# The recurrence's states by single VectorE instructions, smaller quad steps in another order, and new step estimates

## The chip, the cores and the metric

The kernel runs on one core of a Trainium2 chip. The metric is the device time of one execution, in microseconds (us); lower is better. TensorE is called PE here, VectorE DVE, ScalarE ACT, GpSimd POOL, and SyncE, which issues most of the transfers, SP. Each engine takes its instructions strictly in its own order.

## The reference, cut to what matters

One decoder layer on 2048 tokens of width 1024. Eight heads do dilated sliding-window attention in three branches (dilations 1, 4 and 16); eight heads do a gated linear recurrence (HGRN2); both are projected out, and a mixture of 32 experts follows. The change is in the recurrence:

```python
def hgrn2(q, f_raw, i_in, lb):
    """f = lb + (1-lb)*sigmoid(f_raw); S_t = diag(f_t) S_{t-1} + (1-f_t) outer i_t; o_t = S_t^T q_t."""
    ...
    A = jnp.where(causal, jnp.einsum('bnthk,bnshk->bnhts', q_in, k_in), 0.0)
    o_intra = jnp.einsum('bnhts,bnshv->bnthv', A, vc)
    dS = jnp.einsum('bnshk,bnshv->bnhkv', k_end, vc)
    decay = jnp.exp(b_last[:, :, 0])
    def step(S_prev, inp):
        dec, ds = inp
        return dec[..., None] * S_prev + ds, S_prev
    _, S_prevs = lax.scan(step, S0, ...)
    o_inter = jnp.einsum('bnthk,bnhkv->bnthv', q_in, S_prevs)
    return (o_intra + o_inter).reshape(B, S, H, Dv)
```

## The kernel before

The first part (phase A) goes over four **pairs** of heads, each an attention pair with a recurrence pair. On PE a pair consists of: 16 `v` steps (`v_tile`), 32 q/k projection steps (`qk_chunk`), 64 `h` steps (`h_tile`, four to each of 16 token tiles), 48 score steps S (`scores`), 48 value steps P (`values`), and four **quads** of recurrence (`quad_steps`, four tiles each). A quad has the PE steps `decays` (d), `states` (s), `turns` (t), `within` (a) and `outputs` (o), after `gates`, which has no PE work. The second part (phase B, from about 1133 us) projects out and routes; the third (from about 1410 us) runs the experts.

PE's order is the order in which the program is written, and a greedy planner writes it: `Step(fn, cost, after, at)` has an estimated cost and a list of (earlier step, latency) in ns; `Runner.run` keeps a planned time and takes, from lists in a fixed rank (quad steps H first, then weights G, attention A, ..., projections F last), the first step whose predecessors have ended long enough ago. The estimates decide the order alone; at run time semaphores decide. The other engines' orders are made by the framework's scheduler from priorities. `h` steps of quad q wait in the planner for `outputs` of quad q-2 (`hgrn_steps`; `hq` has two buffers).

All quad steps and the weight norms (`w_scale`, PE step w) draw their PSUM tiles from one ring of two banks, `hg`. So a step can start only when the tile before the last one has been read out: by ACT for `states` (dS), `turns` (kT, kept in `key`, and qT) and the two exponentials of `decays`, by DVE for `within` (`copy_predicated` into `Am`).

In `states` each of the two chunks' dS is read out of PSUM by two ACT instructions. Then the recurrence goes eight steps: POOL scales the whole 128x128 state into `sw` (L658), DVE adds dS times the decay in two 64x64 halves (L661), and the next step's POOL instruction needs both. The states lie as 128x128 blocks in `Sp`, whose off-diagonal halves are zero; `outputs` reads `Sp` and `Am`.

`combine` (16 token blocks of branch 2 in pairs, eight calls to a pair of heads) loads the other two branches' rows into `R` by two SP transfers (L506), works on them with DVE (first L511, last L532) and POOL (L529, L531), and stores to `mix` by SP (L534). `R` has two buffers.

## Time and profile before

| what | value |
|---|---|
| median of 3 runs (lowest, highest) | 2217.72 us (2206.78, 2219.48) |
| the profiled execution's own time | 2217.23 us |
| its span, first to last instruction | 2215.3 us |
| mean granted PE clock | 0.943 |

The span lies 1.9 us below the time of the same execution, and that time within 0.5 us of the median. The rows that the prediction uses stand further down. In the strip of slices, each digit is the tenth of a slice (55 us); PEclk is the granted PE clock in tenths of 2.4 GHz, so that 5 is 1.2 GHz.

### The profile page before, as it was taken

Reading aid. Unit: us, or ns where it says so; the run is one execution under the profiler, and the core shown is the slowest. Engines: PE = TensorE matmul, PEld = TensorE weight load, DVE = VectorE, ACT = ScalarE, POOL = GpSimd, SP = SyncE. Lnnn points to the kernel's source line nnn. Section 1 sums busy time; section 2 is a strip of 40 time slices with the busy share of each in tenths; the row PEclk is TensorE's granted clock in tenths of the full one; section 3 lists DMA queues with packets and bytes.
Section 4 is the critical chain, followed back from the end, with each engine's and each line's share of the span. In section 5 each row is a group of like instructions: output and inputs, shape, how many; then the busy total and the mean of one; then the engine's idle time right before and its main releaser. Section 6 shows DMA issues by size and latency. Waiting matters only on the chain. (4 is left out here: it accounts for less than half of the span.)

```text
span 2215.3 us, 39749 instructions
## 1 busy us (share of the span) xinstructions
PE 1967.0 (89%) x13753; PEld 1345.8 (61%) x13777; DVE 1493.8 (67%) x4121; ACT 1201.4 (54%) x2646; POOL 567.3 (26%) x620
## 2 busy tenths in 40 slices
PE   4998978999899998899888998699999999999981
PEld 4645565555655556455444445569999977766750
DVE  6657787767857777567887677756656656556525
ACT  6455653765547655566554343456556655555524
POOL 2303244123431335411431112212233222111110
PEclk9998988998999998999899998799999999999995
DMA  7333254532535324553578995799999999999857
GB/s 229 85 94 96 66 128 112 114 90 70 118 101 123 83 75 113 174 119 71 128 168 226 290 253 164 253 353 315 312 311 314 329 315 313 325 325 321 302 149 299
DMA packets 438896, 433.37 MB, mean 196 GB/s; under 512 B 242644, under 2 KB 325716, under 8 KB 438176
## 3 DMA queue, kind: packets, MB, share of 16 engines
q1 hardware_dynamic: 420464, 382.74, 56.7%
q0 software_dynamic: 14064, 46.46, 8.5%
q8 instruction: 109, 1.79, 0.3%
q10 hardware_dynamic: 4160, 1.58, 0.3%
q14 instruction: 99, 0.81, 0.1%
HBM read 305.30 MB, written 66.29 MB: 168 GB/s over the span
## 5 line engine op out<-in xcount | busy, mean ns | idle before, releaser
L1660 DVE TENSOR_TENSOR eL<-eraw,eH 128x1024 bf16<-128x1024 f32 x248 | 298.0, 1218 | 107.9 <-ACT eH L1654 97.0
L1654 ACT ACTIVATE eH<-eraw 128x1024 fp32r<-128x1024 f32 x252 | 258.4, 1053 | 123.8 <-PE acc L1745 48.8
L453 ACT ACTIVATE P<-S,orow,fqk 128x256 f32<-128x256 f32 (+1 forms) x384 | 195.0, 512 | 172.3 <-DVE orow L447 94.1
L567 PE MATMUL proj<-whh,x 128*128 128x512 f16 x512 | 202.4, 395 | 0.1
L568 PE MATMUL proj<-whl,x 128*128 128x512 f16 x512 | 200.1, 391 | 0.0
L569 PE MATMUL proj<-whh,x 128*128 128x512 f16 x512 | 199.5, 390 | 0.0
L1726 PE MATMUL acc<-xs,eH 128*128 128x352 f32 (+15 forms) x1216 | 195.2, 313 | 1.8 <-DVE xs L1704 1.8
L436 PE MATMUL S<-k,qs 128*128 128x256 f16 (+1 forms) x768 | 172.4, 355 | 13.9 <-ACT P L453 10.9
L1726 PEld LDWEIGHTS acc<-xs,eH 128*128 128x128 f32 x1216 | 176.2, 190 | 4.7 <-issue 2.2
L440 DVE CUSTOM_DVE_ANT_0 S<-S,bias 128x256 f32<-128x256 f32 (+1 forms) x384 | 141.4, 369 | 54.8 <-PE S L436 51.6
L456 DVE TENSOR_TENSOR Ps<-P,Ps 128x256 f16<-128x256 f32 (+1 forms) x192 | 129.7, 675 | 68.8 <-ACT Ps L455 67.2
L1828 POOL DMA_INDIRECT x2d<-yo,sidx x49 | 105.2, 2146 | 255.7 <-DVE yo L1803 95.8
L1776 PE MATMUL acc<-hs,eD 128*128 128x176 f32 (+15 forms) x1216 | 165.1, 295 | 4.9 <-DVE ts L1751 3.0
L1776 PEld LDWEIGHTS acc<-hs,eD 128*128 128x128 f32 x1216 | 161.1, 190 | 6.0 <-DVE ts L1751 3.9
L1687 POOL DMA_INDIRECT xg<-h2d,gidx x49 | 56.1, 1146 | 334.0 <-PE tr L1701 159.6
L436 PEld LDWEIGHTS <-qs 128*128 128x128 f16 x768 | 89.5, 123 | 69.3 <-issue 20.3
L260 POOL TENSOR_TENSOR wraw<-wraw,g 128x1024 f32<-128x1024 f32 x44 | 84.7, 1928 | 167.8 <-DMA wraw<-in_w_in_dram 134.5
L1744 PE MATMUL acc<-eH,xs 128*128 128x512 f32 x208 | 118.4, 569 | 0.0
L1788 PE MATMUL acc<-eD,hs 128*128 128x512 f32 x208 | 98.0, 609 | 21.2 <-ACT yo L1801 11.5
L386 PE MATMUL proj<-wh,x 128*128 128x128 f16 x512 | 96.5, 231 | 18.9 <-DVE V L394 18.9
L455 ACT ACTIVATE Ps<-P 128x256 f16<-128x256 f32 (+1 forms) x192 | 102.8, 536 | 7.6 <-DMA PT<-Ps 5.0
L658 POOL TENSOR_SCALAR sw<-Sp,hw 128x128 f32<-128x128 f32 x112 | 53.3, 476 | 196.5 <-DVE Sp L661 106.5
(396 smaller groups left out, 4891.6 us busy)
## 6 DMA issues: line engine op xcount, KB each, us to landing
eraw<-in_w_gate_dram SPq DMA_DIRECT2D x128, 512.0 KB, 7.1
eD<-in_w_down_dram SPq DMA_DIRECT2D x128, 512.0 KB, 6.4
eraw<-in_w_up_dram SPq DMA_DIRECT2D x124, 512.0 KB, 6.3
wraw<-in_w_in_dram SPq DMA_DIRECT2D x41, 512.0 KB, 4.1
od<-orow SPq DMA_DIRECT2D x64, 132.0 KB, 2.0
R<-od SPq DMA_DIRECT2D x64, 132.0 KB, 2.4
xt<-in_x_dram SPq DMA_DIRECT2D x16, 512.0 KB, 4.8
wraw<-in_w_out_dram SPq DMA_DIRECT2D x16, 512.0 KB, 4.1
```

Source lines behind the costliest of these rows:

```text
L436: nc.tensor.matmul(ps[:, h, :W], q, self.block_cols(D['k'][h][:, x], br, blk, True), start=(x == 0), stop=(x == 1))
L440: nc.vector.tensor_tensor_reduce(ps[:, h, :W], ps[:, h, :W], bias[:, 256 - W:256], 1.0, -3.0e38, OP.add, OP.max, mx[:, h:h + 1])
L453: nc.scalar.activation(P[:, h], ps[:, h, :W], AF.Exp, bias=nm[:, h:h + 1], scale=f[:, h:h + 1], accum_out=orow[:, 130 + h:131 + h])
L456: nc.vector.tensor_tensor(hv[:, 1], P, hv[:, 0], op=OP.subtract)
L567: nc.tensor.matmul(ps, self.XH[n // 4][:, k, ns], W['whh'][:, k, :], start=(k == 0), stop=False)
L568: nc.tensor.matmul(ps, self.XH[n // 4][:, k, ns], W['whl'][:, k, :], start=False, stop=False)
L569: nc.tensor.matmul(ps, self.XL[n // 4][:, k, ns], W['whh'][:, k, :], start=False, stop=(k == KT - 1))
L1654: nc.scalar.activation(H, raw, AF.Copy)
L1660: (nc.gpsimd if on_pool else nc.vector).tensor_sub(L, raw, H.bitcast(F32))
L1726: nc.tensor.matmul(gu[:, i, 0:2 * cap], w[:, o:o + 128], xs[:, k], start=(k == 0), stop=False, skip_group_check=True)
L1744: nc.tensor.matmul(gu[:, j], xs[:, k, 0], H[:, fs], start=(k == 0), stop=False)
L1776: nc.tensor.matmul(py[:, j, 0:cap], W['w_down', f][:, o:o + 128], hs[:, f], start=(f == 0), stop=(f == 3))
```

## The change

Five things are edited.

1. `states` is cut into two steps, one to a chunk. After the second, POOL multiplies both chunks' dS by the following decay (two instructions, 128x256 and 128x192, L654), and the recurrence becomes seven `scalar_tensor_tensor` of 128x64 on DVE (L660) on a compact tile `Sc` (128x8x64, one buffer). The state handed to the next quad is `Send`. Two ACT copies (L666) put the states on the diagonal of `Sp`.
2. `turns` and `within` are cut into two steps each, and the order of the steps in a quad becomes d, t(k), t(q), s0, s1, a0, a1, o instead of d, s, t, a, o.
3. The latencies and costs of these steps are other numbers.
4. In `attention_steps` a score step costs 440, 470 or 930 (430 before), a value step 470 or 240 (330), and a value step follows its score by 15500 (11000).
5. `R` has one buffer instead of two.

```diff
@@ combine
-        R = self.ap_.tile([128, 2, 2, ROW], F32, name="R", bufs=2)
+        R = self.ap_.tile([128, 2, 2, ROW], F32, name="R", bufs=1)
@@ quad_steps
-        def states():
+        def states(ch):
...
-            if q == 0:
-                nc.gpsimd.memset(sp[:, 0], 0.0)
-            else:
-                nc.vector.tensor_scalar(sp[:, 0], sp[:, 8], w[:, 0:1], None, op0=OP.mult)
-            for j in range(1, 8):
-                d = ds[(j - 1) % 2][:, (j - 1) // 2, :]
-                tmp = self.asm.tile([128, 128], F32, name="sw")
-                nc.gpsimd.tensor_scalar(tmp, sp[:, j - 1], w[:, j:j + 1], 1.0, op0=OP.mult, op1=OP.mult)
-                for h in range(2):
-                    hs = slice(64 * h, 64 * h + 64)
-                    nc.vector.scalar_tensor_tensor(sp[hs, j, hs], d[hs], w[hs, j:j + 1], tmp[hs, hs],
-                                                   op0=OP.mult, op1=OP.add)
-            if q < 3:
-                for h in range(2):
-                    hs = slice(64 * h, 64 * h + 64)
-                    nc.gpsimd.tensor_tensor(sp[hs, 8, hs], sp[hs, 7, hs], ds[1][hs, 3], op=OP.add)
+            sc, sp = self.Sc, self.Sp
+            wv = w.rearrange("p (a b) -> p b a", b=2)
+            for ch, n, a in ((0, 4, wv[:, 1]), (1, 3, wv[:, 0, 1:4])):
+                nc.gpsimd.tensor_tensor(ds[ch][:, 0:n], ds[ch][:, 0:n], a[:, :, None].to_broadcast([128, n, 64]), op=OP.mult)
+            if q == 0:
+                nc.vector.memset(sc[:, 0], 0.0)
+            else:
+                nc.vector.tensor_scalar(sc[:, 0], self.Send, w[:, 0:1], None, op0=OP.mult)
+            for j in range(1, 8):
+                nc.vector.scalar_tensor_tensor(sc[:, j], sc[:, j - 1], w[:, j:j + 1], ds[(j - 1) % 2][:, (j - 1) // 2],
+                                               op0=OP.mult, op1=OP.add)
+            if q < 3:
+                nc.vector.tensor_add(self.Send, sc[:, 7], ds[1][:, 3])
+            for h in range(2):
+                hs = slice(64 * h, 64 * h + 64)
+                nc.scalar.activation(sp[hs, :, hs], sc[hs], AF.Copy)
...
         g = Step(gates, 0, [(ready, 1000)])
-        d = Step(decays, 1700, [(g, 14000)])
-        s = Step(states, 1700, [(d, 4000)])
-        t = Step(turns, 900, [(s, 1500)])
-        a = Step(within, 1700, [(t, 2800)])
-        o = Step(outputs, 3400, [(a, 2500), (s, 11000)])
-        return [g, d, s, t, a, o]
+        d = Step(decays, 1600, [(g, 20000)])
+        t0 = Step(lambda: turns(128, "kT"), 450, [(d, 6500)])
+        t1 = Step(lambda: turns(0, "qT"), 450, [(t0, 0)])
+        s0 = Step(lambda: states(0), 720, [(t0, 2500)])
+        s1 = Step(lambda: states(1), 720, [(s0, 0), (t1, 2500)])
+        a0 = Step(lambda: within(0), 720, [(t1, 3500), (s0, 2500)])
+        a1 = Step(lambda: within(1), 720, [(a0, 0), (s1, 2500)])
+        o = Step(outputs, 3700, [(a0, 6000), (a1, 5000), (s1, 9000)])
+        return [g, d, t0, t1, s0, s1, a0, a1, o]
@@ attention_steps
-                S_[i] = Step(lambda i=i: score(i), 430, dep)
+                S_[i] = Step(lambda i=i: score(i), 440 if br == 1 else 470 if br == 2 and blk < 4 else 930, dep)
...
-                dep = [(S_[j], 11000)]
+                dep = [(S_[j], 15500)]
...
-                P_[j] = Step(lambda j=j: value(j), 330, dep)
+                P_[j] = Step(lambda j=j: value(j), 470 if seq[j][1] >= DIL[seq[j][0]] else 240, dep)
```

What this does to the engines' orders is shown at three places, all in the second pair of heads. In the rows, `hg` is the quad's PSUM tile, `sg` holds the quad's decayed q and k, `key` is kT, `S` and `qs`, `k` belong to scores, `O`, `PT` and `V` to values, `proj` and `x` to projections, `orow` is an attention row tile, `mx` its maximum; "..." stands for rows left out.

PE, the second quad (quad 1), from its states (before) or its turns (after) to the start of its outputs. Before:

```order
L643 MATMUL hg<-hq,sg 128x128 x8
...
L672 MATMUL hg<-ct,sg 128x128 x8
...
L683 MATMUL hg<-qT,key 128x128 x8
...
L436 MATMUL S<-k_4443,qs_4331 128x256
...
L569 MATMUL proj<-whh,x_122 128x512
L693 MATMUL hg<-Sp,qT 64x128 x2
```

After:

```order
L671 MATMUL hg<-ct,sg 128x128 x8
...
L642 MATMUL hg<-hq,sg 128x128 x8
...
L436 MATMUL S<-k_4281,qs_4161 128x128
...
L681 MATMUL hg<-qT,key 128x128 x8
...
L436 MATMUL S<-k_4281,qs_4161 128x256
...
L691 MATMUL hg<-Sp,qT 64x128 x2
```

Before, five `h` steps, three scores, three values, the turns and the within stand between states and outputs, and two of the `h` steps right before outputs; after, three scores, three values and the two within steps stand there, no `h` step, and the last of these before outputs is a score. In quad 0 of this pair it is the same: four `h` steps before, none after (three scores, two values). In quads 2 and 3, and at the passage to the next pair, the distances grow: in quad 3 two projection steps stand between within and outputs before, four and a score after.

DVE, the same quad: the end of its recurrence (L661 before, L660 after) among the work of scores (L440, L447) and `copy_predicated` (L684, L682). Before:

```order
L447 TENSOR_TENSOR orow<-mx,fqk 128x2
...
L661 SCALAR_TENSOR_TENSOR Sp<-dS_6070,hw,sw 64x64 x2
L661 SCALAR_TENSOR_TENSOR Sp<-dS_6078,hw,sw 64x64 x2
...
L661 SCALAR_TENSOR_TENSOR Sp<-dS_6070,hw,sw 64x64
...
L684 COPY_PREDICATED Am_104<-cta,hg 128x512
...
L440 ISA S,mx<-S,bias 128x256
```

After:

```order
L440 ISA S,mx<-S,bias 128x256
L440 ISA mx 128x1
L447 TENSOR_TENSOR orow<-mx,fqk 128x2
...
L660 SCALAR_TENSOR_TENSOR Sc<-Sc,hw,dS_6039 128x64
L522 TENSOR_TENSOR den<-den,dent 128x4
L682 COPY_PREDICATED Am_106<-cta,hg 128x512
L523 RECIPROCAL den<-den 128x4
L660 SCALAR_TENSOR_TENSOR Sc<-Sc,hw,dS_6047 128x64
L524 TENSOR_SCALAR den<-den,fqk 128x4
```

Before, the recurrence ends ahead of the work on the first 128x256 score tile; after, its last three instructions stand behind both halves of that tile, the score that stands last before outputs on PE.

SP, the first two calls of `combine` in this pair, with the loads of R and the transposes that feed the values. Before:

```order
L506 DMA R<-od_69 128x264
L458 DMA_TRANSPOSE PT<-Ps 128x4x128 x2
L534 DMA mix<-orow 128x2x128
L506 DMA R<-od_67 128x264
L506 DMA R<-od_69 128x264
L458 DMA_TRANSPOSE PT<-Ps 128x8x128 x2
L534 DMA mix<-orow 128x2x128
```

After:

```order
L506 DMA R<-od_69 128x264
L458 DMA_TRANSPOSE PT<-Ps 128x4x128
L496 DMA od_69<-orow 128x264
L458 DMA_TRANSPOSE PT<-Ps 128x4x128
L458 DMA_TRANSPOSE PT<-Ps 128x8x128
L506 DMA R<-od_67 128x264
L506 DMA R<-od_69 128x264
L534 DMA mix<-orow 128x2x128
```

Before, two calls' loads are issued ahead of the first call's store; after, the second call's loads wait for the first call's last DVE instruction (L532). On DVE the first instruction of a call (L511) now stands 3 to 19 instructions behind the L532 of the call before; before the change it stood ahead of that L532 in most calls.

## Rows read from the trace of the kernel before

**Rows 1.** The page: the span, and two strips of 40 slices.

```profile
span 2215.3 us, 39749 instructions
...
PEclk9998988998999998999899998799999999999995
DMA  7333254532535324553578995799999999999857
```

**Rows 2.** Stretches: us, busy time (and count) by engine, PEclk, DMA share, GB/s.

```profile
core 0: us, PE busy (x) PEld busy (x) DVE busy (x) ACT busy (x) POOL busy (x), PEclk, DMA share, GB/s
121.20:288.60 167.40, 155.28 (x978) 91.17 (x977) 118.88 (x424) 102.21 (x291) 39.35 (x48) 0.94 0.34 83
288.60:386.60 98.00, 75.86 (x727) 54.94 (x725) 77.32 (x220) 46.25 (x110) 45.43 (x49) 0.86 0.51 124
444.60:492.40 47.80, 44.87 (x281) 27.05 (x278) 31.99 (x125) 29.66 (x90) 11.86 (x14) 1.00 0.43 98
492.40:542.40 50.00, 45.24 (x256) 26.09 (x255) 34.64 (x133) 25.92 (x81) 14.39 (x20) 0.86 0.23 59
542.40:585.50 43.10, 40.23 (x259) 22.80 (x256) 41.13 (x159) 27.84 (x75) 18.10 (x25) 0.96 0.45 99
585.50:655.60 70.10, 63.00 (x632) 46.77 (x629) 39.97 (x101) 30.07 (x60) 34.75 (x34) 0.93 0.45 119
713.80:760.50 46.70, 44.87 (x284) 27.07 (x282) 32.85 (x125) 29.78 (x90) 11.86 (x14) 1.00 0.44 100
760.50:809.20 48.70, 43.79 (x256) 25.41 (x255) 34.54 (x134) 25.82 (x81) 14.39 (x20) 0.89 0.24 61
809.20:853.40 44.20, 40.92 (x257) 22.95 (x255) 42.28 (x160) 27.80 (x75) 18.12 (x25) 0.92 0.41 97
853.40:926.50 73.10, 64.26 (x634) 47.39 (x631) 40.96 (x100) 35.85 (x70) 38.99 (x40) 0.91 0.56 157
985.50:1030.60 45.10, 44.42 (x281) 26.88 (x279) 28.57 (x109) 27.54 (x84) 7.61 (x12) 1.00 0.29 76
1030.60:1093.50 62.90, 49.09 (x265) 28.24 (x263) 51.84 (x165) 36.48 (x95) 23.70 (x28) 0.81 0.45 108
```

**Rows 3.** PE's waits, 121 to 1133 us: in total, times, longest.

```profile
PE proj L386 <- DVE V L394: 18.9, 3, 10.9
PE hg L672 <- ACT dS L647: 17.0, 13, 3.0
...
PE hg L697 <- DVE Am L684: 10.3, 4, 5.1
PE hg L615 <- ACT hq L601: 8.8, 4, 3.1
```

**Rows 4.** Groups of instructions on POOL, 0 to 1200 us: busy, mean ns, idle before.

```profile
L658 POOL TENSOR_SCALAR sw<-Sp,hw 128x128 f32<-128x128 f32 x112 | 53.3, 476 | 196.5 <-DVE Sp L661 106.5 <-ACT hw L634 25.0 <-DVE mn L511 17.1
L529 POOL TENSOR_TENSOR R<-R,w 128x256 f32<-128x256 f32 x64 | 43.2, 694 | 85.4 <-DVE w L525 76.5 <-DVE mn L511 4.2 <-issue 3.5
```

**Rows 5.** The same on DVE, 0 to 1200 us.

```profile
L661 DVE SCALAR_TENSOR_TENSOR Sp<-dS,hw,sw 64x64 f32<-64x64 f32 x224 | 74.1, 331 | 29.7 <-POOL sw L658 23.9 <-ACT dS L647 2.2
...
L684 DVE COPY_PREDICATED Am<-cta,hg 128x512 f32<-128x512 int32 x32 | 22.5, 724 | 0.3
```

**Rows 6.** PE in order of time around within, second pair: start, us.

```profile
481.25 1.71 PE L683 MATMUL hg<-qT,key 64*128 64x128 f32 x16
482.89 1.16 PE L436 MATMUL S<-k,qs 128*128 128x128 f16 x4
483.87 0.24 PE L471 MATMUL O<-V,PT 128*128 128x128 f16 x1
...
484.06 0.38 PE L567 MATMUL proj<-whh,x 128*128 128x512 f16 x1
```

**Rows 7.** An ACT copy of the new copies' size, 0 to 1200 us.

```profile
L358 ACT ACTIVATE qs<-proj 64x512 f16<-64x512 f32 x32 | 18.8, 587 | 22.2 <-PE proj L350 17.4 <-DVE qs L359 4.5
```

**Rows 8.** The tile Sp: min/median/max ns of its DVE instruction.

```profile
L661 DVE SCALAR_TENSOR_TENSOR Sp<-dS,hw,sw x224: 245/284/1903, 184.1 to 1188.4; 64x64 f32<-64x64 f32 x112
```

**Rows 9.** The tile R: its loads.

```profile
DMA to landing us min/median/max: 2.0/2.4/4.4
```

More of the change, by code (lines that the diff above doesn't have):

```diff
@@ L659, in states @@
-                for h in range(2):
-                    hs = slice(64 * h, 64 * h + 64)
-                    nc.vector.scalar_tensor_tensor(sp[hs, j, hs], d[hs], w[hs, j:j + 1], tmp[hs, hs],
-                                                   op0=OP.mult, op1=OP.add)
-            if q < 3:
-                for h in range(2):
-                    hs = slice(64 * h, 64 * h + 64)
-                    nc.gpsimd.tensor_tensor(sp[hs, 8, hs], sp[hs, 7, hs], ds[1][hs, 3], op=OP.add)
-        def turns():
-            for o, nm in ((128, "kT"), (0, "qT")):
-                pt = self.psum([128, 4, 128], "hg", 2)
-                for i in range(4):
-                    nc.tensor.transpose(pt[:, i, :], L['sg'][:, i, o:o + 128], c['ident'])
-                t = L[nm] = hp.tile([128, 4, 128], F32, name=("key" if nm == "kT" else nm), bufs=1)
-                nc.scalar.activation(t, pt, AF.Copy)
@@ L676, in within, with turns @@
-        def within():
+                nc.vector.scalar_tensor_tensor(sc[:, j], sc[:, j - 1], w[:, j:j + 1], ds[(j - 1) % 2][:, (j - 1) // 2],
+                                               op0=OP.mult, op1=OP.add)
+            if q < 3:
+                nc.vector.tensor_add(self.Send, sc[:, 7], ds[1][:, 3])
+            for h in range(2):
+                hs = slice(64 * h, 64 * h + 64)
+                nc.scalar.activation(sp[hs, :, hs], sc[hs], AF.Copy)
+        def turns(o, nm):
+            pt = self.psum([128, 4, 128], "hg", 2)
+            for i in range(4):
+                nc.tensor.transpose(pt[:, i, :], L['sg'][:, i, o:o + 128], c['ident'])
+            t = L[nm] = hp.tile([128, 4, 128], F32, name=("key" if nm == "kT" else nm), bufs=1)
+            nc.scalar.activation(t, pt, AF.Copy)
@@ L677, in within @@
+        def within(h):
             qT, kT = L['qT'], L['kT']
             cm = c['causal'].bitcast(I32)[:, None, :].to_broadcast([128, 4, 128])
-            for h in range(2):
-                hs = slice(64 * h, 64 * h + 64)
-                pa = self.psum([128, 4, 128], "hg", 2)
-                for i in range(4):
-                    nc.tensor.matmul(pa[:, i, :], kT[hs, i, :], qT[hs, i, :], start=True, stop=True)
-                nc.vector.copy_predicated(self.Am[h], cm, pa)
+            hs = slice(64 * h, 64 * h + 64)
+            pa = self.psum([128, 4, 128], "hg", 2)
+            for i in range(4):
+                nc.tensor.matmul(pa[:, i, :], kT[hs, i, :], qT[hs, i, :], start=True, stop=True)
+            nc.vector.copy_predicated(self.Am[h], cm, pa)
@@ L744, in phase_a @@
             nc.scalar.dma_start(self.g1, self.aps['norm1_g'][0].rearrange("(t p) -> p t", p=128))
-            self.Sp = apool.tile([128, 9, 128], F32, name="Sp")
+            self.Sp = apool.tile([128, 8, 128], F32, name="Sp")
+            self.Send = apool.tile([128, 64], F32, name="Send")
             nc.vector.memset(self.Sp, 0.0)
@@ L769, in phase_a @@
                 self.ap_ = self.hp = pool("ap", 2)
+                self.Sc = self.hp.tile([128, 8, 64], F32, name="Sc", bufs=1)
                 self.asm = pool("asm", 2)
```

20 lines of the change are left out of this document (10 added, 10 removed).

## The prediction

> **What bounds the kernel now.** I read the page first: the span of 2215.3 us has two kinds of stretches. In the last third the strip of DMA stands at 9 (the experts), and before that, up to about slice 20, it stands at 2 to 5, while the PE clock dips to 8 or 9 of 10 in most slices [rows 1]. So in phase A transfers are no limit, and PE is interrupted often enough to lose clock. The change touches only phase A; what comes after starts when phase A is over, so I take a microsecond won or lost there at its full worth at the end.
>
> Then I read phase A by stretches [rows 2]. For each I take as lost what PE was idle, plus (1 - PEclk) times the length, since at 1.2 GHz, the lower of the clock's two levels, half the work gets done. This is somewhat rough where idle time and low clock coincide. The stretches are cut at PE's landmarks in the pairs numbered 0 to 3:
>
> - pair 0 from its first score to the next pair's first v step: idle 12.1, clock 10.0, lost 22.
> - **boundaries** (v steps and the first half of the q/k projections of pairs 1, 2, 3): 22.1 + 13.7, 7.1 + 4.9, 8.8 + 6.6, lost 36 + 12 + 15 = 63.
> - **quad 0** (tiles 4 to 8, in which quad 0 runs through its chain): lost 3 + 2 + 1 = 6.
> - **quad 1** (tiles 8 to 12): 4.8 + 7.0, 4.9 + 5.4, 13.8 + 12.0, lost 12 + 10 + 26 = 48.
> - **ends** (tile 12 to the next v step, pairs 1 and 2): 2.9 + 1.7 and 3.3 + 3.5, lost 5 + 7 = 12.
>
> That is 151 us, the ceiling of what a better order could win here. What ends PE's waits [rows 3]: the turns wait 13 times (17.0 us) until ACT has read out dS, because the turns' bank is that of the states before; outputs wait for `Am` (10.3); decays wait for the log gates (8.8); and three times a v step waits for the evacuation of V (18.9 us, the longest 10.9).
>
> **The change part by part.** *The recurrence.* It removes 112 POOL instructions of 476 ns, 53.3 us of POOL, which stood waiting for DVE for another 106.5 [rows 4], and halves the 224 DVE instructions of 331 ns; DVE waited 29.7 us ahead of them [rows 5]. It adds 32 POOL multiplies; their nearest row is the 128x256 product on R at 694 ns [rows 4], so about 22 us and certainly not more than the 53.3 removed. It adds 32 ACT copies at 587 ns, the row of a 64x512 copy [rows 7], 19 us on ACT. On DVE, 112 instructions with the same 64 elements in each partition remain, which cost between the 284 ns median [rows 8] and the 331 mean; I take 331, since what made the mean longer is still there. DVE's saving is then 74.1 - 37.1 = 37 us of busy time and up to 29.7 of waiting, over 16 quads 2.3 to 4.2 us each, plus the few small initial and final instructions. None of it is on PE's path by itself: DVE is idle for 13 to 17 us of each 48 to 50 us in the middle of a pair, and nearly full only at the ends and the first boundary (41.13 of 43.1, 77.32 of 98.0) [rows 2].
>
> The chain from states to outputs is what could gain: seven rounds between POOL and DVE become seven DVE instructions. But the order takes away more than the chain gives. Before, in quad 1 of the second pair, five h steps stand between states and outputs; after, none does. PE's own work there is at most three scores of 0.98, the two within steps at 1.64 and three values at 0.19 [rows 6], 5.2 us; in quad 0 it is one value less, 5.0 us. And the order of DVE shows that the last three recurrence instructions now come behind both halves of the score that is PE's last step before outputs. From that score's end DVE has some 15 instructions to do until the last state; at the mean of the stretch (34.64 us over 133, 0.26 us [rows 2]) that is 3.9, with `copy_predicated` at 724 ns among them [rows 5] 4.4. The two copies on ACT add 1.2, together 5.6. The lower bound is 2.5 (scores handled early, copies behind one another at once), the upper 8 (ACT must also finish the exponentials of two scores). I take 5 in quad 1 and 4 in quad 0, where the score tiles are half as wide. This wait is new; behind it in PE's queue stand values and scores, and the h steps that the planner holds back until outputs is done. It also costs clock: a stretch with 4.8 idle lost 7.0 to the clock [rows 2], so between 0 and 7 for each; I take 3.5.
>
> So quad 0 goes from 6 to 3 x 7.5 = 22, a **loss of 16**. In quad 1 the old waits go (decays now stand ten h steps behind the quad's last tile instead of six, and turns no longer stand behind states), and 8.5 each come; in the last pair the output weights are prepared there on ACT, POOL and DVE, and I leave 8 of its excess. 48 becomes 3 x 8.5 + 8 = 34, a **gain of 14**.
>
> *Boundaries.* Idle time is 38.0 of the 63, V's wait 18.9 of that, so by share 31 belongs to V and 32 to quad steps that stand too close. In quad 3 the distances grow (within to outputs from two projection steps to four and a score). I leave 9 of the 32. V waits because DVE is full; one quad's 4 us less of DVE there takes off 5 of 31. **Gain 23 + 5 = 28.** Should DVE stay the limit there, it is 0; should V's wait go too, 50.
>
> *Ends and pair 0.* At the ends the turns' wait for dS goes; 12 becomes 8, **gain 4**. Pair 0 has the same new quads 0 and 1; 22 becomes 20, **gain 2**.
>
> *R with one buffer.* The loads of a `combine` now wait for L532 of the call before: two issues and a landing of 2.4 us [rows 9], about 3.4 in all. On DVE, L511 stands 3 to 19 instructions behind that L532, mostly 8, which is 2.9 us at 0.36 us from one to the next (48.7 us over 134 [rows 2]). So DVE stands still for half a microsecond in most of 28 calls, 15 to 20 us, most of it where DVE has idle time: **5 us lost**. Between 0 and 48. SP isn't held longer than before, since the store of the same call, which waits for the same instruction, already stood in its queue.
>
> *Value steps 15500 behind their scores.* Rows 3 leave no large wait of values to win; nothing.
>
> The sum: 2217.2 - 28 + 16 - 14 - 4 - 2 + 5 = 2190. The profiled execution is within 0.5 us of the median, so this holds for the median too.
>
> **The rivals.** *The chain is short.* If ACT, POOL and DVE finish the states before PE has done its 5 us, the new waits vanish: 3 x 7.5 + 3 x 8.5 = 48 more, 2142. For it speaks that the seven instructions alone take 2.3 us; against it the place of the last three in DVE's order. *DVE stays full at the boundaries.* Then their 28 don't come: 2218, no change. For it: 77.32 of 98.0 busy, and scores and combines there are as many as before. *R decides.* Where L511 stands in the middle of the recurrence (in quad 1 it does), a late load stops the states, and outputs with them. If all 28 calls wait the full 3.4 us, 95 us, and half of it reaches PE, that is 48 instead of 5: 2233, slower. It decides from the point where fewer than about 9 DVE instructions stand between L532 and the next L511, which holds for half of the calls; against it, DVE's idle quarter takes up much.
>
> One rule of the Trainium skill speaks against the new form. A recurrence instruction lost 47 ns of its mean against the median, though single ones took up to 1903 ns [rows 5, 8]. The page SBUF — State Buffer, section Who interferes with whom, says that a VectorE instruction with two SBUF inputs can't share the second read port with a GpSimd instruction that reads SBUF; whoever comes second waits for the whole of the other. L660 has two such inputs, as L661 had. If by this rule each of the six chains above met one such case of 1.6 us, the time would be 2200; the mean in the row says that it is rare.
>
> **How the numbers follow.** 1% here is 22 us, about what a measurement of this kernel can tell from no change, so the border is 2195. The sum with its likeliest bounds (waits of 3 to 7 us, 15 to 40 at the boundaries) runs from 2170 to 2210: chance 0.45, of which 0.28 is faster and 0.17 within 1%. The short chain: 0.22, all faster. DVE stays full: 0.16, within. R decides: 0.17, slower. Together faster 0.50, same 0.33, slower 0.17. A range for 8 in 10 leaves out part of the short chain and part of the slow case: 2146 to 2230.
>
> **What would show it.** In the profile after: PE's waits on dS at the turns and on the log gates gone; a new wait of PE at the first `outputs` matmul, 4 to 5 us long, in quads 0 and 1 of each pair, on ACT's copy into `Sp`; the chain from the first to the last L660 still 6 us or longer; L511 waiting for the load of R; the boundary stretches shorter by 5 to 12 us each. I would be wrong if the chain is done before the last score (then faster), or if the boundaries keep their idle time.

## The result and the profile after

The changed kernel takes **2288.5 us** (median of 4 runs, 2286.5 to 2291.2) against 2215.2 of the kernel before (4 runs): ratio **1.0336, 95% interval 1.0306 to 1.0366**, slower by some 73 us. The forecast was 2190, the range 2146 to 2230.

First the page of the kernel after, its span and the same two strips as in [rows 1]:

```profile
span 2286.5 us, 39485 instructions
...
PEclk9997888979999789898787999699999999999995
...
DMA  7234154532535325443347998599999999999957
```

The last third is as it was. The loss lies in the first half, where the clock now shows 7 and 8 in many slices. The stretches of the kernel after answer to [rows 2], cut at the same landmarks of PE (pair 1: quad 0, quad 1, end; then quad 0 of pairs 2 and 3, and the last quad 1):

```profile
core 0: us, PE busy (x) PEld busy (x) DVE busy (x) ACT busy (x) POOL busy (x), PEclk, DMA share, GB/s
...
445.00:503.60 58.60, 49.98 (x293) 30.39 (x292) 33.84 (x120) 34.95 (x96) 9.75 (x8) 0.82 0.42 87
503.60:555.20 51.60, 45.95 (x267) 27.70 (x266) 28.77 (x115) 30.21 (x88) 10.05 (x10) 0.87 0.21 52
555.20:596.20 41.00, 38.14 (x239) 21.45 (x238) 32.67 (x126) 22.61 (x65) 13.58 (x15) 1.00 0.44 94
596.20:682.30 86.10, 67.14 (x658) 49.05 (x657) 54.47 (x155) 38.71 (x87) 34.95 (x33) 0.90 0.43 108
...
1030.20:1083.70 53.50, 49.45 (x294) 30.86 (x293) 30.59 (x109) 35.45 (x96) 6.90 (x7) 0.84 0.38 92
1083.70:1148.80 65.10, 49.28 (x267) 29.34 (x266) 37.57 (x121) 35.60 (x94) 15.38 (x14) 0.74 0.33 82
```

Quad 0 of pair 1, 47.8 us before at full clock, takes 58.6 with 8.6 idle and a clock of 0.82. Set against [rows 2] by the prediction's parts:

| part | forecast | measured | lengths before, after |
|---|---|---|---|
| quad 0, pairs 1 to 3 | +16 | **+31.0** | 47.8, 46.7, 45.1; 58.6, 58.5, 53.5 |
| quad 1, pairs 1 to 3 | -14 | **+7.0** | 50.0, 48.7, 62.9; 51.6, 51.9, 65.1 |
| ends | -4 | -4.6 | 43.1, 44.2; 41.0, 41.7 |
| pair 0 | -2 | +8.6 | 167.4; 176.0 |
| first v step to tile 4, pairs 1 to 3 | -28 | **+16.8** | 156.0, 128.3, 132.1; 151.3, 139.0, 142.9 |
| ahead of the first score | - | -3.5 | 121.2; 117.7 |
| from tile 12 of pair 3 to the end | - | +15.9 | 1121.8; 1137.7 |

The sum is +71.2, the difference of the spans. For the boundaries the second half of the projections is counted too, since three scores have moved from it into the first. PE's waits after, 60 to 1250 us, answer to [rows 3]:

```profile
PE hg L691 <- ACT Sp L666: 51.9, 12, 6.9
PE proj L386 <- DVE V L394: 16.0, 2, 8.2
PE proj L567 <- ACT hq L574: 13.4, 4, 8.0
PE proj L348 <- DVE V L394: 12.8, 4, 4.7
...
PE hg L642 <- ACT qT L673: 6.8, 4, 2.2
PE hg L642 <- ACT key L673: 6.7, 4, 3.0
```

The turns' waits on dS are gone, those of the decays on the log gates too. In their place the states (L642) wait 13.5 us until ACT has read out qT and kT: with two banks, whichever comes second waits. Outputs wait 51.9 us for the copies into `Sp`, and for V two kinds of steps now wait, 28.8 us in all (18.9 before). The instructions themselves cost about what was forecast. Groups on DVE, ACT and POOL after, 0 to 1250 us:

```profile
L660 DVE SCALAR_TENSOR_TENSOR Sc<-Sc,hw,dS 128x64 f32<-128x64 f32 x106 | 34.8, 328 | 15.5 <-POOL dS L654 14.8
...
L666 ACT ACTIVATE Sp<-Sc 64x512 f32<-64x512 f32 x30 | 18.8, 627 | 11.0 <-DVE Sc L660 10.4
...
L654 POOL TENSOR_TENSOR dS<-dS,hw 128x256 f32<-128x256 f32 (+1 forms) x31 | 17.6, 569 | 141.2 <-ACT dS L646 141.1 <-DMA PT<-Ps 0.2
```

They were taken at 331, 587 and 694 ns, the last for the larger of its two forms. So no operation was priced too low by much; what went wrong is where they stand. PE in order of time in quad 0 of pair 1 (start, length, line):

```profile
478.62 0.38 PE L569 MATMUL proj<-whh,x 128*128 128x512 f16 x1
...
487.21 1.11 PE L436 MATMUL S<-k,qs 128*128 128x128 f16 x4
494.56 0.69 PE L691 MATMUL hg<-Sp,qT 128*64 128x128 f32 x4 [6.23 <-ACT Sp L666]
...
496.23 0.70 PE L691 MATMUL hg<-Sp,qT 128*64 128x128 f32 x4
...
503.63 0.60 PE L567 MATMUL proj<-whh,x 128*128 128x512 f16 x1
```

The last h step of tile 7 ends at 479.0, the next h step, tile 8's first, comes at 503.6. For 24.6 us PE has none, only scores, values and the quad's own steps; between the same two steps it went 6.9 us without one before, and in [rows 6] an h step came a microsecond after `within`. Here is what ran on the other engines in that time (DVE and ACT, thinned out):

```profile
484.95 0.35 DVE L660 SCALAR_TENSOR_TENSOR Sc<-Sc,hw,dS 128x64 f32<-128x64 f32 x1
...
488.15 1.05 ACT L606 ACTIVATE sg<-sg 128x1024 f32<-128x1024 f32 x1
488.47 0.30 DVE L440 CUSTOM_DVE_ANT_0 S<-S,bias 128x128 f32<-128x128 f32 x1 [0.86 <-PE S L436]
...
491.93 0.28 DVE L660 SCALAR_TENSOR_TENSOR Sc<-Sc,hw,dS 128x64 f32<-128x64 f32 x1
...
492.93 0.62 ACT L666 ACTIVATE Sp<-Sc 64x512 f32<-64x512 f32 x1
493.45 0.41 ACT L455 ACTIVATE Ps<-P 128x256 f16<-128x256 f32 x1
493.88 0.63 ACT L666 ACTIVATE Sp<-Sc 64x512 f32<-64x512 f32 x1
```

Seven instructions of 0.28 us take 7.0 us from first start to last, because score work stands between them, among it scores that PE hasn't done yet. Exponentials of scores stand ahead of the first copy, and a copy of score work (L455) between the two.

### The profile page after: what moved, and what is told of

The parts are those of the page before. It is cut to its first block, busy times and chain, and to the rows that moved or that the text cites. A ratio compares the mean times of both kernels' runs of the same rounds, so it can differ in the third digit from the quotient of the medians.

```text
span 2286.5 us, 39485 instructions
## 1 busy us (share of the span) xinstructions
PE 1999.1 (87%) x13777; PEld 1368.0 (60%) x13777; DVE 1456.6 (64%) x4025; ACT 1224.8 (54%) x2678; POOL 522.9 (23%) x512
## 5 line engine op out<-in xcount | busy, mean ns | idle before, releaser
L1658 ACT ACTIVATE eH<-eraw 128x1024 fp32r<-128x1024 f32 x252 | 258.2, 1053 | 116.2 <-PE acc L1749 47.8
L440 DVE CUSTOM_DVE_ANT_0 S<-S,bias 128x256 f32<-128x256 f32 (+1 forms) x384 | 140.8, 370 | 106.3 <-PE S L436 103.7
L436 PEld LDWEIGHTS <-qs 128*128 128x128 f16 x768 | 82.2, 125 | 52.7 <-issue 14.5
L348 PE MATMUL proj<-x,wh 128*128 128x512 f16 x256 | 102.1, 399 | 13.1 <-DVE V L394 12.8
L455 ACT ACTIVATE Ps<-P 128x256 f16<-128x256 f32 (+1 forms) x192 | 102.5, 534 | 4.9 <-DMA PT<-Ps 2.3
```

What stands on the lines that cost most here:

```text
L436: nc.tensor.matmul(ps[:, h, :W], q, self.block_cols(D['k'][h][:, x], br, blk, True), start=(x == 0), stop=(x == 1))
L440: nc.vector.tensor_tensor_reduce(ps[:, h, :W], ps[:, h, :W], bias[:, 256 - W:256], 1.0, -3.0e38, OP.add, OP.max, mx[:, h:h + 1])
L1658: nc.scalar.activation(H, raw, AF.Copy)
```

## Theories and experiments

**Interleaving**: outputs wait because the recurrence is spread over other work. **Ring**: the new latencies make a quad's planned chain longer (from the gates to the end of outputs, adding the latencies and costs in `quad_steps`: 35.8 us before, 45.2 after). The h steps of quad q wait in the planner for outputs of quad q-2, so PE runs out of h steps before outputs come. **R**: with one buffer the calls of `combine` follow one another; that paces them and carries DVE work into the boundaries, where V's evacuation stands behind it. **Lag**: the value steps at 15500 do that.

Ratios below are to the kernel before on the same chip; 1% is 22.1 us, and a step from one kernel to another is the difference of their ratios.

| kernel | median us | ratio (95% interval) |
|---|---|---|
| changed | 2288.5 | 1.0336 (1.0306 to 1.0366) |
| a_two_R | 2264.0 | 1.0235 (1.0187 to 1.0283) |
| a_old_estimates | 2255.6 | 1.0213 (1.0187 to 1.0239) |
| a_late_outputs | 2248.6 | 1.0188 (1.0171 to 1.0206) |
| a_chain_first | 2238.3 | 1.0129 (1.0112 to 1.0146) |
| a_gates_14000 | 2226.4 | 1.0054 (1.0031 to 1.0077) |
| a_gates_old_est | 2224.7 | 1.0060 (1.0040 to 1.0080) |
| a_turns_4000 | 2219.5 | 1.0040 (1.0021 to 1.0060) |
| a_gates_old_first | 2214.3 | 1.0019 (1.0006 to 1.0032) |
| b_est_only | 2266.5 | 1.0242 (1.0194 to 1.0290) |
| b_turns_first | 2244.4 | 1.0132 (1.0087 to 1.0176) |
| b_one_R | 2237.5 | 1.0126 (1.0079 to 1.0173) |
| b_turns_apart | 2213.7 | 1.0006 (0.9985 to 1.0026) |
| b_gates_20000 | 2213.4 | 0.9994 (0.9976 to 1.0013) |
| b_rec_only | 2195.7 | 0.9931 (0.9907 to 0.9955) |
| b_chain_first | 2179.5 | 0.9844 (0.9802 to 0.9886) |
| **b_states_first** | **2175.0** | **0.9862 (0.9827 to 0.9898)** |

### The parts alone

**b_rec_only**: the kernel before with the recurrence of the change (L651 to L666, `Sc`, `Send`); `both` calls the halves one after the other, so that the steps and R are as before.

```diff
-        s = Step(states, 1700, [(d, 4000)])
-        t = Step(turns, 900, [(s, 1500)])
-        a = Step(within, 1700, [(t, 2800)])
+        s = Step(lambda: both(states, (0,), (1,)), 1700, [(d, 4000)])
+        t = Step(lambda: both(turns, (128, "kT"), (0, "qT")), 900, [(s, 1500)])
+        a = Step(lambda: both(within, (0,), (1,)), 1700, [(t, 2800)])
```

> The kernel before with the new recurrence alone (L654 to L666), PE's order, the estimates and two buffers of R as before. Theory order: the new waits come from where outputs stand, not from the instructions; then this is no slower than before, 2205 to 2217, and outputs wait less than 10 us for the copies into Sp. Rival, chain: one engine's chain is held up by other DVE and ACT work wherever outputs stands; then outputs wait 20 us or more here too and the time is above 2230.

15 us faster than before, more than theory order had (2205 to 2217). Outputs wait once for the copies, 0.6 us. The new recurrence is a gain in the order of before, where h steps stand ahead of outputs.

**a_two_R** and **b_one_R**: one number, each way.

```diff
-        R = self.ap_.tile([128, 2, 2, ROW], F32, name="R", bufs=1)
+        R = self.ap_.tile([128, 2, 2, ROW], F32, name="R", bufs=2)
```

> The changed kernel with two buffers of R again. Theory R: one buffer makes the combine calls follow one another at some 11.5 us (first L511 to first L511 at the second boundary), which carries 24 to 35 more DVE instructions of them into each boundary, and V's evacuation, for which PE waits, stands behind them. Then the waits at the boundaries of the last two pairs shrink to those of before, 25 to 35 us are gained, 2255 to 2263; the waits of outputs on the copies into Sp (51.9 us) stay. Rival, lag: the calls stand late because a value step follows its score by 15500 instead of 11000; then at most 8 us come back, 2280 or more.

> The kernel before with one buffer of R, nothing else. Theory R: slower by 20 to 35 us, 2235 to 2250, most of it at the boundaries by V's evacuation. Rival, lag: without the longer lag of the value steps one buffer costs 0 to 8, 2215 to 2223. My recorded term for it was 5 us.

Taking the single buffer away gives 22 us, adding it to the kernel before costs 28. The first and last L511 of pair 1 show the pace, for the kernel after, with two buffers, and for the kernel before with one:

```profile
L511 DVE TENSOR_TENSOR mn<-orow,R x8: 148/162/615, 533.0 to 636.1; 128x4 f32<-128x4 f32 x8
```

```profile
L511 DVE TENSOR_TENSOR mn<-orow,R x8: 148/162/558, 527.4 to 610.7; 128x4 f32<-128x4 f32 x8
```

```profile
L511 DVE TENSOR_TENSOR mn<-orow,R x8: 148/160/1226, 511.3 to 613.4; 128x4 f32<-128x4 f32 x8
```

From the first L511 to the eighth it takes 103 us with one buffer, 83 with two, and 102 in the kernel before once it has one (80.7 with two): R sets the pace, whatever the lag, and the rival's 2280 is out. In b_one_R the two stretches from the first v step to tile 4 of pairs 2 and 3 grow from 128.3 and 132.1 to 142.2 and 145.3 us, 27 in all. But V's evacuation isn't the way there: the waits for V are 3.9 and 2.8 us at these two boundaries, 3.6 and 4.4 before. The new waits of some size are those of the quad's steps on DVE (for `Am` 4.6 us and for `seq` 4 at each). In a_two_R only some 13 of its 22 come from there (151.3, 139.0, 142.9 to 144.0, 134.5, 141.3), 8 from the last part; the waits for V fall there from 28.8 to 10.7, and still the boundaries stay longer than before, so R alone doesn't explain them.

**b_est_only**: the kernel before with the score and value estimates of the change.

```diff
-                dep = [(S_[j], 11000)]
+                dep = [(S_[j], 15500)]
...
+                S_[i] = Step(lambda i=i: score(i), 440 if br == 1 else 470 if br == 2 and blk < 4 else 930, dep)
+                P_[j] = Step(lambda j=j: value(j), 470 if seq[j][1] >= DIL[seq[j][0]] else 240, dep)
```

> The kernel before with the new estimates of score and value steps alone (score 440, 470 or 930, value 470 or 240, lag 15500). Theory lag: the values and so the combine calls come some 4 us later at each pair's end, V's waits grow, and planned time passes faster for the quads, so that fewer h steps stand between their steps: slower by 10 to 30, 2225 to 2245. Theory R or order alone: within 8 us of before. My recorded term for it was nothing.

Slower by 54 us, more than I expected of it. In the profile the boundaries grow by 47 us and the stretch from tile 12 of the last pair to the end by 35; most of the rest gets shorter. PE also waits 21.0 us for the log gates (8.8 before), but that this is the reason isn't shown. What the estimates cost inside the change is another matter; the next group tells it.

### Inside the changed kernel, with two buffers of R

**a_late_outputs** and **a_chain_first**:

```diff
-        o = Step(outputs, 3700, [(a0, 6000), (a1, 5000), (s1, 9000)])
+        o = Step(outputs, 3700, [(a0, 6000), (a1, 5000), (s1, 14000)])
```

```diff
+            with self.tc.high_priority(offset=AHEAD):
+                sc, sp = self.Sc, self.Sp
...
+                    nc.scalar.activation(sp[hs, :, hs], sc[hs], AF.Copy)
```

> The changed kernel with two buffers of R and outputs 14000 behind the second states step instead of 9000. Theory wait: PE stands at outputs because they are placed one or two scores too early; moved back, the 55.0 us of waits on the copies into Sp fall below 15, and 30 us or more come back, 2235 or less. Rival, ring: the h steps of the quad after next wait for outputs in the planner (two buffers of hq), so that PE has run out of them by then and only scores are left; the wait falls all the same, but the later outputs hold the h steps back by as much: 2260 to 2275, no gain.

> The changed kernel with two buffers of R and the whole recurrence (the two POOL products, the seven DVE instructions, the two ACT copies) ahead in the framework's priorities, PE's order unchanged. Theory wait by interleaving: DVE's score work between the recurrence's instructions and ACT's exponentials ahead of the copies make the chain last 12.8 us; with priority the waits on Sp fall from 55.0 to 25 or less, and 20 to 30 us come back, 2235 to 2245. Rival: the chain is limited by what feeds it (dS on ACT) or pushes the scores back as far as it comes forward; waits on Sp 40 or more, 2258 or more.

With outputs later, PE's waits are these, and quad 0 takes 57.9, 57.2 and 54.6 us in pairs 1 to 3, about as long as in a_two_R (58.3, 58.2, 52.8):

```profile
PE proj L567 <- ACT hq L574: 31.5, 7, 7.1
PE S L436 <- ACT P L453: 26.9, 22, 2.8
...
PE hg L691 <- ACT Sp L666: 8.4, 8, 2.0
```

```profile
436.00:493.90 57.90, 51.60 (x310) 31.83 (x309) 34.53 (x135) 38.76 (x107) 9.13 (x8) 0.90 0.42 93
```

47 of 55 us of waiting on `Sp` vanish and the quads don't get shorter. 33 us of it come back elsewhere: h steps wait 31.5 us until ACT has read out the tile before into `hq` (13.9 in a_two_R), scores 26.9 for the exponentials (11.7). PE goes as long without an h step as before, 23.3 us in pair 1. So the wait was the place where the lack of h steps showed, not its cause, as the ring has it. What the kernel gains, 10 us by the ratios, lies in the main at the boundaries (134.5 and 141.3 us to 123.0 and 131.9 from the first v step to tile 4 in pairs 2 and 3, less 8 at the ends); its total stands between the two expectations.

With priority, the chain of quad 0 in pair 1 runs from 473.96 to 478.24 (its first and last instruction here), 4.3 us instead of 7.0, and the copies go back to back:

```profile
473.96 0.35 DVE L661 SCALAR_TENSOR_TENSOR Sc<-Sc,hw,dS 128x64 f32<-128x64 f32 x1
...
478.24 0.28 DVE L661 SCALAR_TENSOR_TENSOR Sc<-Sc,hw,dS 128x64 f32<-128x64 f32 x1
...
478.55 1.27 ACT L667 ACTIVATE Sp<-Sc 64x512 f32<-64x512 f32 x2 [0.33 <-DVE Sc L661]
```

Waits on `Sp` fall from 55.0 to 19.0 and 23 us come back: interleaving is a cost of its own. PE's order is the same; a faster chain brings outputs, and with them the h steps behind them, forward in time (20.9 us without an h step instead of 24.5).

**a_gates_14000**, **a_old_estimates**: the two sets of numbers, one at a time.

```diff
-        d = Step(decays, 1600, [(g, 20000)])
+        d = Step(decays, 1600, [(g, 14000)])
```

```diff
-                S_[i] = Step(lambda i=i: score(i), 440 if br == 1 else 470 if br == 2 and blk < 4 else 930, dep)
+                S_[i] = Step(lambda i=i: score(i), 430, dep)
-                dep = [(S_[j], 15500)]
+                dep = [(S_[j], 11000)]
-                P_[j] = Step(lambda j=j: value(j), 470 if seq[j][1] >= DIL[seq[j][0]] else 240, dep)
+                P_[j] = Step(lambda j=j: value(j), 330, dep)
```

> The changed kernel with two buffers of R and one number of its quad steps as before: decays 14000 behind the gates instead of 20000. In PE's order two to three h steps then stand between the second states step and outputs of quads 0 and 1, where there was none. Theory ring (the planned chain of a quad is longer than the h steps that fill it, and the h steps after next wait for outputs): the stretch from tile 4 to tile 8 of the second and third pair falls from 58.3 and 58.2 us to 50 to 54, waits on Sp below 15, 2225 to 2240. Rival, the gates aren't ready: decays wait for the log gates 3 us or more in each quad, and the stretch stays above 55: 2255 or more.

> The changed kernel with two buffers of R and the score and value estimates of before (430, 330, 11000); the quad steps in the new order with the new latencies remain. Theory: the estimates cost the 50 us that they cost when added alone; then this is at 2215 or below. Rival, ring: the new latencies make the planned chain of a quad 45 us instead of 36, longer than the 16 h steps that fill it; outputs still wait 35 us or more on Sp, and it stays at 2235 or above.

14000 brings 40 us, although PE now waits for the log gates, 43.4 us in ten times. Quad 0 falls to 54.4, 47.6 and 48.1 us, 19 in all, and PE goes 7.2 us without an h step there in pair 1 instead of 24.5. The row of pair 2:

```profile
710.90:758.50 47.60, 42.82 (x282) 25.81 (x280) 33.14 (x110) 31.74 (x85) 9.71 (x8) 1.00 0.41 98
```

Quad 1 gains more, 33 us in the three pairs, and pair 0 18; the boundaries and the stretch from tile 12 of the last pair to the end lose 38. The old estimates bring 5 us, inside the intervals; outputs still wait 43.9. So the lag and the costs together are not what makes the change slow, and the ring's expectation held. The 5 us are a difference of large terms, though: with the old estimates pair 0 and quad 1 of the three pairs are 42 us longer, and boundaries, ends and the last stretch 54 shorter (15 of them in the last stretch, 1129.8 to 1114.5).

**a_gates_old_est**, **a_gates_old_first**, **a_turns_4000**: both diffs above at once; then also the recurrence ahead; then, without that, the turns nearer to decays.

```diff
-        t0 = Step(lambda: turns(128, "kT"), 450, [(d, 6500)])
+        t0 = Step(lambda: turns(128, "kT"), 450, [(d, 4000)])
```

> The changed kernel with two buffers of R, the score and value estimates of before, and decays 14000 behind the gates. Of the change remain the recurrence, the turns ahead of the states at 6500 and outputs at 9000. Theory ring: the 14000 brings some 38 us against the kernel with the old estimates alone (2255.6), and with the old estimates the log gates are ready: waits on them below 15, 2200 to 2222. Rival, place of the turns: with turns ahead of states it stays at 2235 or more, as the kernel with states first did when its turns were put ahead (2244.4).

> The kernel of the label a_gates_old_est with the recurrence ahead in the priorities as well. Theory: R, the distance from the gates, the estimates and the interleaved chain are the four costs; without them this lies at 2180 to 2205, near the kernel with the recurrence alone (2195.7). Rival: a fifth cost, the turns ahead of the states, holds 20 us or more: 2215 or more.

> The kernel of the label a_gates_old_est with the turns 4000 behind decays, where states stood before, instead of 6500. Theory ring: another 2.5 us per quad of planned chain goes, 5 to 15 us faster than that kernel. Rival: the factors eq and ek aren't ready, the turns wait 2 us or more each, and the time is the same within 5 or longer.

The first takes off 34 us against a_old_estimates and ends 3 above its forecast; the second takes 9 more and ends at 2214, next to its rival's bound and 35 us above the best kernel: a fifth cost is left, in the steps' order. The turns' distance is not it (4 us, intervals overlap). It only moves the loss: in a_turns_4000 quad 0 takes 46.9, 45.8 and 44.7 us, as in the best kernel (52.2, 51.2 and 53.0 with 6500), and quad 1 56.1, 53.5 and 67.9 (46.3, 45.2 and 66.1).

### From the other side: the kernel before with the recurrence

**b_states_first**: steps cut in two as in the change, but states ahead of the turns, and outputs 9000 behind the states as in the change (11000 before).

```diff
+        d = Step(decays, 1700, [(g, 14000)])
+        s0 = Step(lambda: states(0), 850, [(d, 4000)])
+        s1 = Step(lambda: states(1), 850, [(s0, 0)])
+        t0 = Step(lambda: turns(128, "kT"), 450, [(s0, 2500)])
+        t1 = Step(lambda: turns(0, "qT"), 450, [(s1, 2500)])
+        a0 = Step(lambda: within(0), 850, [(t1, 2800)])
+        a1 = Step(lambda: within(1), 850, [(a0, 0)])
+        o = Step(outputs, 3700, [(a1, 2500), (s1, 9000)])
```

> The new recurrence with two buffers of R and the old estimates, the quad steps cut in two as in the change, but in the order d, s0, s1, t0, t1, a0, a1, o with latencies near those of before (14000 from the gates, 9000 from states to outputs), so that other work stands between the turns and the states. Theory: the turns' waits on dS (14.0 us in the kernel with the recurrence alone) go, outputs come a little earlier, 2180 to 2195. Rival: those waits lay beside others (V's evacuation, the log gates) and come back there; 2195 to 2205.

2175, faster than both kernels and than I expected. Waits of the turns on dS fall from 14.0 in b_rec_only to 8.8, and quad 0 runs at full clock, with h steps up to outputs:

```profile
467.96 0.38 PE L567 MATMUL proj<-whh,x 128*128 128x512 f16 x1
468.87 0.44 PE L691 MATMUL hg<-Sp,qT 128*64 128x128 f32 x4
...
469.82 0.44 PE L691 MATMUL hg<-Sp,qT 128*64 128x128 f32 x4
```

```profile
428.40:474.90 46.50, 44.77 (x284) 27.17 (x281) 31.27 (x119) 32.19 (x93) 9.56 (x7) 1.00 0.51 103
```

**b_gates_20000**, **b_turns_first**, **b_turns_apart**, **b_chain_first** each put one part of the change into it.

```diff
-        d = Step(decays, 1700, [(g, 14000)])
+        d = Step(decays, 1700, [(g, 20000)])
```

```diff
+        t0 = Step(lambda: turns(128, "kT"), 450, [(d, 4000)])
+        t1 = Step(lambda: turns(0, "qT"), 450, [(t0, 0)])
+        s0 = Step(lambda: states(0), 850, [(t0, 2500)])
+        s1 = Step(lambda: states(1), 850, [(s0, 0), (t1, 2500)])
```

```diff
+        a0 = Step(lambda: within(0), 850, [(t1, 2800), (s0, 2500)])
+        a1 = Step(lambda: within(1), 850, [(a0, 0), (s1, 2500)])
```

The first diff is b_gates_20000, the second b_turns_first, the second and third together b_turns_apart; b_chain_first has the recurrence ahead in priority, as above.

> The kernel with states first (2175.0 us) and one number of the change in it: decays 20000 behind the gates instead of 14000. Theory ring: quad 0's outputs come after the h steps have run out; the stretch from tile 4 to tile 8 (46.5 us there) grows by 4 to 10 in each pair, quad 1's too, and the time by 25 to 50: 2200 to 2225. Rival: the distance only saves waits on the log gates (6.3 us there) and PE fills it with scores: 2170 to 2185.

> The kernel with states first (2175.0 us) but the turns ahead of the states, as in the change; the latency from the gates stays 14000. Theory: states, and with them the recurrence and outputs, come some 4 us later, but h steps still stand ahead of outputs, so little is lost: 2175 to 2195, waits on Sp below 10. Rival, order: the turns' place is what costs the change its time: 2215 or more.

> The kernel of the label b_turns_first (2244.4 us, within waits 29.4 us for dS) with the within steps also 2500 behind their states step, as the change has it; turns still ahead of states. Theory place: the turns ahead put states and the recurrence 3.4 to 4 us later in each quad, which the serial chain of quads pays for: against states first (2175.0) 15 to 40 us remain, 2190 to 2215. Rival, bank: all of the 69 us were the two-bank ring between states and within; without those waits 2175 to 2188. Second rival: nothing of it was the ring, 2235 or more.

> The kernel with states first (2175.0 us) with the recurrence ahead in the framework's priorities; PE's order is the same. Theory: where outputs have h steps ahead of them the chain isn't waited for (no wait on Sp among the large ones), so priority gains nothing: 2170 to 2182. Rival: the states finish just as outputs come, and priority frees 10 us or more: 2165 or less.

20000 alone costs 29 us, as the ring has it, but not where I expected it first: quad 0 grows by 1.7, 0.9 and 3.9 us only, quad 1 by 5.4, 8.4 and 6.2, pair 0 by 12.5 and the boundary of pair 3 by 11. The time that PE goes without an h step shows the ring directly. In pair 1 it is 6.1 us in b_states_first until tile 8 begins and 1.1 until tile 12; with 20000 it is 12.7 and 16.3, in the changed kernel 24.6 and 20.8. The turns ahead cost 60, far over what I expected; 28 of them are the two banks (`within` waited 29.4 us for dS, and with 9.3 of that left the time is 2213.7), 32 remain. In the profile 25 lie in quad 1: from tile 8 to tile 12 the three pairs take 48.0, 55.7 and 62.4 us against 45.2, 42.2 and 53.9, while quad 0 stays within 0.6. Pair 0 adds 12 and the boundary of pair 3 15, and the ends give 13 back. What holds quad 1 there I could not settle: in pair 3 outputs wait once 10.2 us for a `combine` in DVE's order, and of 11.4 us of waits for `Sp` in seven places 5.9 lie in quad 1 of pair 2. Priority for the recurrence changes nothing (0.9844 against 0.9862, the intervals overlap): a chain that nobody waits for needn't be shorter.

A third buffer for `hq`, which would open the ring directly, was not tried.

## Why the prediction was wrong, step by step

By the parts of the table and the 5 us set aside for R the forecast missed by 98 us: 45 at the boundaries, 21 in quad 1, 15 in quad 0, 16 at the end, 11 in pair 0, less 9 for the rest. The way from the best kernel to the changed one, in single steps: turns ahead of states +32 us; turns at 6500 and the other latencies and costs of the quad's steps +12 (a_gates_old_est); decays at 20000 +34; the estimates +5, not told from nothing; one R +22. Together 105 us; against them stand the 30 us between the kernel before and the best one, 15 for the recurrence alone and 15 for the steps cut in two with states first. The sizes hold for this sequence: 20000 cost 29 and 40 us in two other places, the estimates 54 on the kernel before.

*Quad 0, where the first step failed.* The size of the new wait was about right: 4 to 5 us forecast, 6.23 and its like measured, made as I had said by the last recurrence instructions behind a score and the copies behind exponentials. What failed is "behind it in PE's queue stand values and scores, and the h steps that the planner holds back until outputs is done": I named the h steps and priced them at nothing. I counted PE's work between states and outputs, 5 us, and not what PE had lacked since the last h step, 24.6 us filled with scores that come no faster than DVE and ACT take them. So in pair 1 the idle time is 8.6 instead of 4 and the clock term 0.18 x 58.6 = 10.5 instead of 3.5. By the prediction's measure the three quads lose 19 + 19 + 13 = 51 us instead of 22; their lengths grew by 31 instead of 16. The measure itself is too large here, partly since it counts idle time at the low clock twice.

*Quad 1.* That decays stand "ten h steps behind the quad's last tile instead of six" I took for a cure of the waits on the log gates. It is: they are gone. But it is also the longer chain that exhausts the h steps, and the 48 us lost became 58 (idle plus clock: 12 and 33 from the rows above, 13 in pair 2) instead of 34. b_gates_20000 and a_gates_14000 show both sides: 29 and 40 us for that one number; in the profiles quad 1 alone changes by 20 and 33. That "turns no longer stand behind states" saved little: now the states wait behind the turns, 13.5 us after 17.0.

*Boundaries, where the second step failed.* I let larger distances take 23 us off and V's wait 5, as if nothing else of the change came there. Something of that gain exists: with two buffers of R and the old estimates (a_old_estimates) the boundaries are 15 us shorter than before. The new estimates add 18 and the one R 13, and -28 became +17. V's wait grew from 18.9 to 28.8, because `combine` moved in: between the first v step and the second half of the projections DVE is busy 54.47 us in pair 2, 39.97 before [rows 2]. "V waits because DVE is full" was read too broadly: 39.97 of 70.1 us isn't full. What counts is what stands ahead of V's evacuation in DVE's order; after the change, between 610 and 625 us, DVE is busy 13.45 of 15.

*R.* I took 5 us from half a microsecond a call, hidden where DVE is idle (28 calls make 14 us of that, not the 15 to 20 that I wrote); the rival took 48 for stops on PE's path. It is 22 to 28, by a third way. DVE does stand still for the loads, 25.7 us in 27 places and 3.1 at most, but above all each call ends before the next begins, and the calls slide into the boundary, ahead of work that PE waits for. The bound 0 to 48 held, the value didn't.

*Value steps at 15500.* Priced at nothing, and with the new costs not told from nothing inside the change, by luck: terms of some 50 us cancel. The pairs' last values and scores come later, into the boundary. After the last pair 15.9 us appear that I hadn't priced at all; a_old_estimates takes 15.3 off there, a_two_R 7.8. That late quads have no cover there would be a reason, but isn't shown.

*The recurrence, ends.* The recurrence was priced right, 328 ns for 331; alone it is worth 15 us. The short-chain rival was true of it in the order of before (0.6 us of waits) and false of the change. The ends came out at -4.6 for -4 by luck: the turns' waits on dS went (2.5 and 2.4 us), but the states wait 2.2 and 2.1 there for qT.

*The port rule.* By the Trainium skill (SBUF — State Buffer, Who interferes with whom) a VectorE instruction with two SBUF inputs and a GpSimd instruction that reads SBUF wait for one another. The trace agrees that it happens; here are the two engines in the kernel after, at two places:

```profile
296.25 1.89 POOL L260 TENSOR_TENSOR wraw<-wraw,g 128x1024 f32<-128x1024 f32 x1
296.33 1.90 DVE L660 SCALAR_TENSOR_TENSOR Sc<-Sc,hw,dS 128x64 f32<-128x64 f32 x1
298.28 0.27 DVE L660 SCALAR_TENSOR_TENSOR Sc<-Sc,hw,dS 128x64 f32<-128x64 f32 x1
...
612.84 1.90 POOL L260 TENSOR_TENSOR wraw<-wraw,g 128x1024 f32<-128x1024 f32 x1 [6.18 <-DVE den L524]
612.85 1.91 DVE L525 TENSOR_TENSOR w<-w,den 128x12 f32<-128x12 f32 x1
...
617.10 2.10 DVE L532 TENSOR_TENSOR orow<-orow,R 128x256 f32<-128x256 f32 x1 [0.66 <-POOL R L531]
```

DVE's first instruction, whose next one takes 0.27 us, lasts as long as POOL's and ends 0.09 us after it. I had set 2200 for this case of the recurrence. Of its 112 instructions 19 overlap a POOL instruction, with a mean of 556 ns against 279, 5 us of DVE in all: there it doesn't decide. But at the boundary it falls on `combine`, which stands ahead of V's evacuation at 622.00: L525 takes 1.91 us (0.17 in most calls) and L532 2.10 (0.43). Between 596.2 and 682.3 us the instructions of `combine` that overlap POOL's take 11 us more than their medians, at the boundary before 2.4. What that costs in time was not tested.

## What to carry to other kernels

Where a planner spaces a chain by latencies and other work waits for the chain's end by a buffer, price a longer latency by the work that then runs out, not by the wait at the chain's end: moving the waiting step away removes the wait and not the loss. A buffer taken away costs the overlap of whole calls, and the bill comes where they slide ahead of work that somebody waits for. Make such changes one at a time: here the recurrence alone won 15 us, and states first 15 more, while the other order, the numbers and the missing buffer lost 105.

## What the runs showed of the hardware

A stretch with little work for PE costs beyond its idle time, by the granted clock. Outputs after the 6.23 us take 1.67 us for a tile (494.56 to 496.23 above), in the kernel with states first 0.95 (468.87 to 469.82). The clock there is 0.50, the lower of its two levels, and 1.00, the higher; the last column but two of these rows (the first two of the kernel after, the third of b_states_first):

```profile
484.00:488.00 4.00, 4.00 (x32) 3.20 (x32) 3.58 (x14) 3.94 (x10) 1.04 (x2) 0.79 0.15 33
496.20:501.00 4.80, 4.80 (x25) 3.55 (x25) 0.00 (x0) 0.00 (x0) 0.00 (x0) 0.50 0.22 2
468.80:472.80 4.00, 4.00 (x37) 3.00 (x34) 1.04 (x2) 2.39 (x7) 0.00 (x0) 1.00 0.29 69
```

In the kernel after the clock fell between 484 and 488 us, and the wait begins at 488.3. So the wait isn't what lowered it: PE had done no h step since 479.0, only scores, values and the quad's own steps, with hardly a gap in their records. In b_gates_20000 PE goes 12.7 us without an h step up to 487.8, and the clock is 1.00 from 439.6 to there. I hadn't expected that moving outputs back doesn't bring the clock back: in a_late_outputs PE waits 1.07 us at outputs and 2.35 ahead of the last score, the clock is 0.50 from 484.8 on, and a tile of outputs takes the same 1.67:

```profile
482.64 1.11 PE L436 MATMUL S<-k,qs 128*128 128x128 f16 x4 [2.35 <-ACT P L453]
484.83 0.70 PE L691 MATMUL hg<-Sp,qT 128*64 128x128 f32 x4 [1.07 <-ACT Sp L666]
...
486.50 0.70 PE L691 MATMUL hg<-Sp,qT 128*64 128x128 f32 x4
```
